# A transformer-like layer on one core: both token halves normed first, and modulated in turn after each half of the modulation vectors

## The chip, the core and the metric

The kernel runs on one core of a Trainium2 chip. TensorE (PE) multiplies matrices, VectorE (DVE) and ScalarE (ACT) do elementwise work, GpSimd (POOL) helps with a few subtractions, and SyncE (SP) issues the DMA transfers from one queue. The metric is device time in microseconds; three runs of the kernel before gave 1233.12 to 1235.85 with a median of 1234.98.

## The reference

One layer of a streaming encoder, 1024 tokens of width 1024, all in float32. Only its beginning matters here:

```python
mod = silu(c) @ w_ada + b_ada                      # 6 vectors of 1024
shift1, scale1, gate1, shift2, scale2, gate2 = split(mod, 6)
u = layer_norm(x) * (1 + scale1) + shift1
proj = u @ w_in                                    # columns: rq rk rv rg gq gk gv gg glr
m = token_mixer(proj) @ w_out                      # retention heads and gated linear attention
x = layer_norm(alpha * x + gate1 * m, ln1)
...                                                # second modulation, relu(.)**2 feed-forward, second norm
```

`c` is a single vector, so `mod` is a matrix-vector product that reads all of `w_ada`, 25 MB.

## The kernel before

The kernel is written as a program whose instructions a scheduler puts in order on each engine; the order of the code, priorities and the buffers that tiles share decide it. `tc.issue_after(i)` lets what is written inside it be placed only behind instruction i. Every engine then runs its own queue strictly in that order, and semaphores hold an instruction until what it reads has been written.

Tokens are worked on in two halves h of 512 (four tiles of 128 each), features in eight blocks k of 128. `load_x` (line 295) issues eight loads of 256 KB for a half; `ln_x` (307) takes statistics on VectorE, gets the scale `rs` and bias `nb` for four tiles at once (a square root on ScalarE in the middle), writes the normed tiles `xh` (six on ScalarE, two on VectorE), transposes them on TensorE in eight groups of four (line 331) and copies each group to SBUF on ScalarE as `xT[k][h]` (334).

The first modulation (shift1 and scale1) is computed in two halves b of 512 columns each, by `ada_first` (251). A half loads 16 weight tiles of 256 KB. For the first `share` of the eight row blocks, TensorE multiplies the tile by a column of silu(c) (line 262); the rest are summed on VectorE into `acc` (235 and 237), and one matmul adds the partitions of that sum. ScalarE copies the two result rows (264), four tiny transposes turn them (267), and VectorE adds the bias into `mod` (269). With SHARES = ((8, 0), (6, 0)), half 0 has nine such matmuls and half 1 has eight.

`modulate_all(h, b)` then makes, for the four feature blocks of half b, `uf` = xT * scale + shift on VectorE (341) and splits it into a rounded part `uh` (cast on ScalarE, 204) and a remainder `ul` (subtraction on VectorE, 205). A float32 product is three matmuls of such parts (`mm3`, 210 to 212). `begin(h, keys)` starts the products of three key and query blocks (gq 0, gk 0, gq 1) with the first four feature blocks of a half: 36 matmuls of 512 columns. The other four blocks follow in `feature_major` (430) when the second half of the modulation is done, and after gq 0 and gk 0 come the gv products (`values_and_gate`, 454).

PSUM is used through two pools of four buffers each, `pj` and `mx`; the transposes and the modulation sums take theirs from `mx`. The code that sets the order of the beginning stands at lines 405 to 422.

Of the kernel before, what the change touches and what calls it, by code (L numbers as in the profile page):

```python
# [78 lines left out]
def layer_kernel(ctx: ExitStack, tc, x, c, w_ada, b_ada, w_in, ret_norm_w, gla_gate_w, gla_gate_b,  # L79
# [27 lines left out]
    def S(shape=(P, HALF), dt=F32, n="s"):  # L107
        tag, bufs = TAGS.get(n, ("S", None))
        return sp.tile(list(shape), dt, tag=tag, name=nm(n), bufs=bufs)
# [7 lines left out]
    def pjt(shape=(P, HALF)):  # L117
        return pj.tile(list(shape), F32, tag="pj", name=nm("pj"))

    def mxt(shape=(P, HALF)):  # L120
        return mx.tile(list(shape), F32, tag="mx", name=nm("mx"))

    def small(n, tag, bufs=4):
        return sm.tile([P, n], F32, tag=tag, name=nm(tag))
# [51 lines left out]
    def row_rsqrt(dst, var, n=1):  # L176

        v, y, t = small(n, f"qv{n}"), small(n, f"qy{n}"), small(n, f"qt{n}")
        A.activation(y, var, AF.Sqrt, bias=eps)
        V.tensor_scalar(out=v, in0=var, scalar1=EPS, scalar2=None, op0=ALU.add)  # L180
        yield
        V.reciprocal(out=y, in_=y)
        yield
        if n == 1:

            V.tensor_scalar(out=t, in0=y, scalar1=-0.5, scalar2=y, op0=ALU.mult, op1=ALU.mult)
            V.tensor_scalar(out=t, in0=t, scalar1=v, scalar2=None, op0=ALU.mult)
            yield
            V.tensor_scalar(out=dst, in0=t, scalar1=1.5, scalar2=y, op0=ALU.add, op1=ALU.mult)
            return  # L190
        V.scalar_tensor_tensor(out=t, in0=y, scalar=-0.5, in1=y, op0=ALU.mult, op1=ALU.mult)
        V.tensor_tensor(out=t, in0=t, in1=v, op=ALU.mult)
        yield
        V.scalar_tensor_tensor(out=dst, in0=t, scalar=1.5, in1=y, op0=ALU.add, op1=ALU.mult)

    def stats(parts, mv):
        bs = small(6 * len(parts), f"bs{len(parts)}")
        for i, a in enumerate(parts):
            V.bn_stats(out=bs[:, 6 * i:6 * i + 6], in_=a)
        V.bn_aggr(out=mv, in_=bs)  # L200
# [6 lines left out]
    def mm3(ps, lh, ll, rh, rl, first, last, partial=False):  # L207


        T.matmul(ps, lhsT=lh, rhs=rh, start=first, stop=False, skip_group_check=partial)  # L210
        T.matmul(ps, lhsT=lh, rhs=rl, start=False, stop=False, skip_group_check=partial)  # L211
        T.matmul(ps, lhsT=ll, rhs=rh, start=False, stop=last, skip_group_check=partial)  # L212
# [10 lines left out]
    def ada_load(cols, get):  # L223
        ws = []
        for k in range(NK):
            w = get()
            nc.sync.dma_start(out=w, in_=wa[k, :, cols:cols + HALF])
            ws.append(w)
        return ws

    def ada_sum(ws, ks):
        acc = S(n="acc")
        for n, k in enumerate(ks):
            if n == 0:
                V.tensor_scalar(out=acc, in0=ws[k], scalar1=sc[:, k:k + 1], scalar2=None, op0=ALU.mult)
            else:
                V.scalar_tensor_tensor(out=acc, in0=ws[k], scalar=sc[:, k:k + 1], in1=acc, op0=ALU.mult, op1=ALU.add)
        return acc
# [12 lines left out]
    def ada_first(b, shares):  # L251


        ps = mxt()
        todo = []
        for i, share in ((1, shares[0]), (0, shares[1])):
            ws = ada_load(1024 * i + HALF * b, ada_early)
            todo += [(pick2[:, 16 * i + 2 * k:16 * i + 2 * k + 2], ws[k]) for k in range(share)]
            if share < NK:
                todo.append((pick2[:, 32 + 2 * i:34 + 2 * i], ada_sum(ws, range(share, NK))))  # L260
        for n, (l, r) in enumerate(todo):
            yield T.matmul(ps[0:2, :], lhsT=l, rhs=r, start=n == 0, stop=n == len(todo) - 1)
        r = S(n="acc")
        A.copy(out=r[0:2, :], in_=ps[0:2, :])
        pt = mxt((P, 4, 2))
        for j in range(4):
            T.transpose(out=pt[:, j, :], in_=r[0:2, j * P:(j + 1) * P], identity=ident[0:2, 0:2])
        for i in range(2):
            V.scalar_tensor_tensor(out=mod[:, 8 * i + 4 * b:8 * i + 4 * b + 4], in0=pt[:, :, i], scalar=float(i),
                                   in1=colT[:, 8 * i + 4 * b:8 * i + 4 * b + 4], op0=ALU.add, op1=ALU.add)  # L270
# [24 lines left out]
    def load_x(h):  # L295
        xs = []
        for j in range(4):
            t = 4 * h + j
            pr = []
            for q in range(2):  # L300
                a = S(n="x")
                nc.sync.dma_start(out=a, in_=x[0, t * P:(t + 1) * P, q * HALF:(q + 1) * HALF])
                pr.append(a)
            xs.append(pr)
        return xs

    def ln_x(h, xs):
        mv = small(8, "mvx", bufs=2)
        for j in range(4):
            stats(xs[j], mv[:, 2 * j:2 * j + 2])  # L310
        mvv = mv.rearrange("p (j two) -> p j two", two=2)
        rs = small(4, "rsx", bufs=2)
        nb = small(4, "nbx", bufs=2)
        var = small(4, "varx", bufs=2)
        V.tensor_copy(out=var, in_=mvv[:, :, 1])
        for _ in row_rsqrt(rs, var, 4):
            pass
        V.scalar_tensor_tensor(out=nb, in0=mvv[:, :, 0], scalar=-1.0, in1=rs, op0=ALU.mult, op1=ALU.mult)
        hs = [[None, None] for _ in range(4)]
        for q in range(2):  # L320
            for j in range(4):
                a = hs[j][q] = S(n="xh")
                if q == 0 and j % 2:
                    V.tensor_scalar(out=a, in0=xs[j][q], scalar1=rs[:, j:j + 1], scalar2=nb[:, j:j + 1],
                                    op0=ALU.mult, op1=ALU.add)
                else:
                    A.activation(a, xs[j][q], AF.Identity, bias=nb[:, j:j + 1], scale=rs[:, j:j + 1])
        for k in range(NK):
            ps = mxt()
            for j in range(4):  # L330
                T.transpose(out=ps[:, j * P:(j + 1) * P], in_=hs[j][k // 4][:, (k % 4) * P:(k % 4 + 1) * P],
                            identity=ident)
            xT[k][h] = S(n="xT")
            A.copy(out=xT[k][h], in_=ps)
# [4 lines left out]
    def modulate(k, h, src, sh, s1):  # L339
        u = S(n="uf")  # L340
        V.tensor_scalar(out=u, in0=src, scalar1=s1, scalar2=sh, op0=ALU.mult, op1=ALU.add)
        uh[k][h] = S(dt=F32R, n="uh")
        ul[k][h] = S(dt=F32R, n="ul")
        split(u, uh[k][h], ul[k][h], lo_eng=V)
# [21 lines left out]
    for kind in ("gqk0", "gqk1", "rqk0", "rqk1", "rqk2", "rqk3"):  # L366
        i = int(kind[3])
# [13 lines left out]
    def take(key, ahead=1):  # L381

        n = order.index(key)
        for u in order[:n + 1 + ahead]:
            if u not in loaded:
                loaded[u] = load_w(*W[u])
        return loaded[key]

    def begin(h, keys):

        for key in keys:
            w = take(key, 0)
            begun.setdefault(key, [None, None])[h] = ps = pjt() if key[1] == 0 else mxt()
            for k in range(4):
                mm3(ps, w[0][k], w[1][k], uh[k][h], ul[k][h], k == 0, False)

    begun = {}
    SHARES = ((8, 0), (6, 0))
    EARLY_KEYS = (("gq", 0), ("gk", 0), ("gq", 1))

    def modulate_all(h, b):
        for k in range(4 * b, 4 * b + 4):
            modulate(k, h, xT[k][h], mod[:, k:k + 1], mod[:, 8 + k:9 + k])

    xs = load_x(0)
    steps = ada_first(0, SHARES[0])
    for _ in range(SHARES[0][0]):
        i = next(steps)
    with tc.issue_after(i.ins):
        ln_x(0, xs)  # L410
    for _ in steps:
        pass
    modulate_all(0, 0)
    begin(0, EARLY_KEYS)
    ln_x(1, load_x(1))
    for i in ada_first(1, SHARES[1]):
        pass
    modulate_all(1, 0)
    with tc.issue_after(i.ins):
        begin(1, EARLY_KEYS)  # L420
    for h in range(2):
        modulate_all(h, 1)
    nc.sync.dma_start(out=cst1, in_=cst[:, C_DEC:])
# [732 lines left out]
    ys, x1, xs = {}, {}, {}  # L1156
# [79 lines left out]
    for t in range(NT):  # L1236
        tile_steps = final(t)
        for step in range(4):
            i = next(tile_steps)
# [34 lines left out]
```

## Time and profile before

| | us |
|---|---|
| median of three runs | 1234.98 |
| profiled execution | 1232.21 |
| its span | 1230.4 |
| TensorE busy | 1170.1 (95%) |
| VectorE busy | 959.5 (78%) |
| ScalarE busy | 495.4 (40%) |

The page lists for each engine how long it was busy in the span, and then the span in 40 slices; the timeline lists single instructions in order of time; the windows give the busy time of an engine in stretches. PEclk is the clock that TensorE was granted, as a share of full speed (2.4 GHz). The first slice of 31 us and the last hold the least TensorE work; the DMA engines are busy for over 90% of the first.

### The profile page before, as it was taken

How to read it: one execution, taken by the hardware profiler on the slowest of the kernel's cores; microseconds unless marked ns; L12 is line 12 of the kernel's file. 1: busy time of each engine (PE TensorE's matmuls, PEld its weight loads, DVE VectorE, ACT ScalarE, POOL GpSimd, SP SyncE). 2: the span in 40 equal slices, each digit the busy share in tenths (PEclk: the TensorE clock that was granted, in tenths of full speed). 3: DMA queues.
4: the chain of work that ended last, by engine and by line, in shares of the span. 5: the costliest groups of instructions: out<-in, count | busy, mean ns of one | idle time of the engine just before them, and what ended most of it. 6: DMA issues, size and time to landing. Idle time of an engine off the chain costs nothing. (4 is left out here: it accounts for less than half of the span.)

```text
span 1230.4 us, 19534 instructions
## 1 busy us (share of the span) xinstructions
PE 1170.1 (95%) x7195; PEld 973.8 (79%) x7195; DVE 959.5 (78%) x1870; ACT 495.4 (40%) x887; POOL 162.1 (13%) x141
## 2 busy tenths in 40 slices
PE   5899889989999999999989999999999999999995
PEld 2588788759989999888867887888887888878784
DVE  6885888888776763698898799864856976897886
ACT  5514333211222232223754457756655363431132
POOL 0000332041000000000000000000002131243146
PEclk9999999989999999999999999999999999999998
DMA  9793211110110313181236688563656275378442
GB/s 314 248 332 120 87 61 36 28 27 18 44 36 25 101 64 95 60 273 44 94 112 208 209 306 308 195 210 130 224 188 204 78 254 156 114 236 299 174 137 103
DMA packets 124129, 183.13 MB, mean 149 GB/s; under 512 B 12337, under 2 KB 52482, under 8 KB 124034
## 3 DMA queue, kind: packets, MB, share of 16 engines
q1 hardware_dynamic: 124034, 181.89, 44.5%
q8 instruction: 56, 0.92, 0.3%
q14 instruction: 39, 0.32, 0.1%
HBM read 136.76 MB, written 45.09 MB: 148 GB/s over the span
## 5 line engine op out<-in xcount | busy, mean ns | idle before, releaser
L211 PE MATMUL pj<-wl,uh 128*128 128x256 f32 (+1 forms) x512 | 146.8, 287 | 1.0 <-DVE wl L205 1.0
L212 PE MATMUL pj<-wh,ul 128*128 128x256 f32 (+1 forms) x512 | 146.9, 287 | 0.0
L210 PE MATMUL pj<-wh,uh 128*128 128x256 f32 (+1 forms) x512 | 146.5, 287 | 0.3 <-ACT wh L204 0.3
L210 PE MATMUL pj<-uhp,w1h 128*128 128x512 f32 x256 | 100.9, 396 | 1.7 <-ACT w1h L204 1.1
L210 PE MATMUL pj<-bh,ah 128*128 128x512 f32 x256 | 99.9, 391 | 1.6 <-DVE yacc L1100 1.6
L211 PE MATMUL pj<-ulp,w1h 128*128 128x512 f32 x256 | 100.4, 393 | 0.1
L212 PE MATMUL pj<-uhp,w1l 128*128 128x512 f32 x256 | 100.4, 393 | 0.0
L211 PEld LDWEIGHTS pj<-wl,uh 128*128 128x128 f32 x512 | 98.2, 192 | 2.2 <-DVE wl L205 1.2
L212 PE MATMUL pj<-bh,al 128*128 128x512 f32 x256 | 99.7, 390 | 0.0
L211 PE MATMUL pj<-bl,ah 128*128 128x512 f32 x256 | 99.7, 389 | 0.0
L210 PEld LDWEIGHTS pj<-wh,uh 128*128 128x128 f32 x512 | 98.0, 192 | 1.2 <-ACT wh L204 0.7
L212 PEld LDWEIGHTS pj<-wh,ul 128*128 128x128 f32 x512 | 98.2, 192 | 1.0 <-issue 0.7
L205 POOL TENSOR_TENSOR al<-rh,ah 128x512 fp32r<-128x512 f32 x17 | 26.9, 1580 | 537.4 <-PE pj L212 474.5
L210 PE MATMUL mx<-bh,ah 128*128 128x512 f32 x192 | 75.6, 395 | 3.5 <-ACT bh L204 2.4
L210 PE MATMUL mx<-uhp,w1h 128*128 128x512 f32 x192 | 75.6, 395 | 2.9 <-ACT w1h L204 2.7
L211 PE MATMUL mx<-bl,ah 128*128 128x512 f32 x192 | 75.4, 393 | 1.5 <-POOL bl L205 1.3
L212 PE MATMUL mx<-uhp,w1l 128*128 128x512 f32 x192 | 75.7, 395 | 0.0
L211 PE MATMUL mx<-ulp,w1h 128*128 128x512 f32 x192 | 75.6, 394 | 0.0
L212 PE MATMUL mx<-bh,al 128*128 128x512 f32 x192 | 75.3, 392 | 0.0
L205 DVE TENSOR_TENSOR w1l<-raw,w1h 128x512 fp32r<-128x512 f32 x80 | 54.7, 686 | 25.6 <-ACT w1h L204 16.1
L210 PE MATMUL pj<-uh,wh 128*128 128x512 f32 x176 | 71.3, 406 | 1.6 <-ACT uh L204 1.6
L204 ACT CAST ah<-rh 128x512 fp32r<-128x512 f32 x84 | 51.9, 618 | 51.3 <-PE pj L211 21.4
(256 smaller groups left out, 2874.8 us busy)
## 6 DMA issues: line engine op xcount, KB each, us to landing
raw<-in_w_ff SPq DMA_DIRECT2D x140, 256.0 KB, 4.3
ada<-in_w_ada SPq DMA_DIRECT2D x96, 256.0 KB, 5.4
rh<-hid SPq DMA_DIRECT2D x84, 256.0 KB, 3.7
hid<-c SPq DMA_DIRECT2D x54, 256.0 KB, 2.6
st<-in_w_in SPq DMA_DIRECT2D x52, 256.0 KB, 3.0
hid<-m SPq DMA_DIRECT2D x30, 256.0 KB, 2.2
hid<-kl SPq DMA_DIRECT2D x28, 256.0 KB, 3.0
hid<-kh SPq DMA_DIRECT2D x28, 256.0 KB, 2.9
```

Source lines behind the costliest of these rows:

```text
L204: A.copy(out=hi, in_=src)
L205: (lo_eng or G).tensor_tensor(out=lo, in0=src, in1=hi.bitcast(F32), op=ALU.subtract)
L210: T.matmul(ps, lhsT=lh, rhs=rh, start=first, stop=False, skip_group_check=partial)
L211: T.matmul(ps, lhsT=lh, rhs=rl, start=False, stop=False, skip_group_check=partial)
L212: T.matmul(ps, lhsT=ll, rhs=rh, start=False, stop=last, skip_group_check=partial)
```

## The change

The two halves of x are loaded and normed ahead of everything else. Then comes the first half of the modulation, the modulation of both token halves by it, each followed by its 36 products, and then the second half of the modulation. The `issue_after` orderings of this part are gone. Functions and shares stay as they are; after.py's lines from 411 on have numbers that are 6 lower.

```diff
-    xs = load_x(0)
-    steps = ada_first(0, SHARES[0])
-    for _ in range(SHARES[0][0]):
-        i = next(steps)
-    with tc.issue_after(i.ins):
-        ln_x(0, xs)
-    for _ in steps:
+    xs = [load_x(h) for h in range(2)]
+    for h in range(2):
+        ln_x(h, xs[h])
+    for _ in ada_first(0, SHARES[0]):
         pass
-    modulate_all(0, 0)
-    begin(0, EARLY_KEYS)
-    ln_x(1, load_x(1))
-    for i in ada_first(1, SHARES[1]):
+    for h in range(2):
+        modulate_all(h, 0)
+        begin(h, EARLY_KEYS)
+    for _ in ada_first(1, SHARES[1]):
         pass
-    modulate_all(1, 0)
-    with tc.issue_after(i.ins):
-        begin(1, EARLY_KEYS)
     for h in range(2):
         modulate_all(h, 1)
```

How the queues change is seen at three places. In the names a number tells tiles of one kind apart: `ada` is a weight tile of the modulation, `acc` a VectorE sum of such tiles or the copied result row, `xh` a normed tile, `xT` a transposed block, `wh` and `wl` the two parts of a weight.

TensorE, around the sums of the first modulation half, before:

```order
L262 MATMUL mx_113<-ada_114,pick_92 2x512
...
L262 MATMUL mx_113<-ada_128,pick_92 2x512
L331 MATMUL mx_210<-keep,xh_194 128x128
...
L331 MATMUL mx_259<-keep,xh_208 128x128
L262 MATMUL mx_113<-acc_146,pick_92 2x512
L267 MATMUL mx_269<-keep,acc_267 128x2 x4
L210 MATMUL pj_312<-uh_278,wh_302 128x512
```

and now:

```order
L331 MATMUL mx_176<-keep,xh_160 128x128
...
L331 MATMUL mx_225<-keep,xh_174 128x128
L331 MATMUL mx_279<-keep,xh_263 128x128
...
L331 MATMUL mx_328<-keep,xh_277 128x128
L262 MATMUL mx_335<-ada_336,pick_92 2x512
...
L262 MATMUL mx_335<-acc_368,pick_92 2x512
L267 MATMUL mx_388<-keep,acc_386 128x2 x4
L210 MATMUL pj_431<-uh_397,wh_421 128x512
```

The eight sums stood ahead of half 0's transposes; now the transposes of both halves (`xh_160` to `xh_174` are half 0, `xh_263` to `xh_277` half 1) stand ahead of all nine.

TensorE, around the sums of the second modulation half, before:

```order
L331 MATMUL mx_487<-keep,xh_436 128x128
L262 MATMUL mx_494<-ada_495,pick_92 2x512
...
L262 MATMUL mx_494<-acc_530,pick_92 2x512
L210 MATMUL pj_580<-uh_558,wh_302 128x512
...
L267 MATMUL mx_549<-keep,acc_547 128x2 x4
L211 MATMUL pj_580<-ul_565,wh_302 128x512
...
L212 MATMUL mx_606<-uh_576,wl_353 128x512
L210 MATMUL pj_312<-uh_621,wh_308 128x512
```

and now:

```order
L212 MATMUL mx_481<-uh_415,wl_472 128x512
L210 MATMUL pj_518<-uh_496,wh_421 128x512
...
L212 MATMUL mx_544<-uh_514,wl_472 128x512
L262 MATMUL mx_557<-ada_558,pick_92 2x512
...
L262 MATMUL mx_557<-acc_593,pick_92 2x512
L267 MATMUL mx_612<-keep,acc_610 128x2 x4
L210 MATMUL pj_431<-uh_621,wh_427 128x512
```

Half 1's 36 products stood between the sums and the first product of the second half of the features (`uh_621`); now they stand ahead of the sums, and between the sums and `uh_621` there are only the four tiny transposes.

ScalarE, behind the copies of half 0's transposes, before:

```order
L334 COPY xT_264<-mx_259 128x512
L204 CAST wh_302<-st_300 128x512
L264 COPY acc_267<-mx_113 2x512
L204 CAST wh_308<-st_306 128x512
L204 CAST uh_278<-uf_276 128x512
```

and now:

```order
L334 COPY xT_230<-mx_225 128x512
L179 ACTIVATE qy_62_254<-varx_251,keep 128x4
L327 ACTIVATE xh_263<-x_113,nbx_250,rsx_249 128x512
...
L334 COPY xT_284<-mx_279 128x512
...
L334 COPY xT_333<-mx_328 128x512
L204 CAST wh_421<-st_419 128x512
...
L264 COPY acc_386<-mx_335 2x512
L204 CAST uh_397<-uf_395 128x512
```

Half 1's square root, six normed tiles and eight copies, and six casts of weights, now stand between half 0's last copy and the copy of the modulation's result row. On SP, 14 of the 16 x loads stand ahead of the first weight load of the modulation, and the last x load is the 21st of the large loads.

## Rows read from the trace of the kernel before

**Rows 1.** Windows: start and end, length, PE busy, PEclk, DMA share, GB/s.

```profile
0.00:75.00 75.00, 56.88 (x228) 0.95 0.89 295
75.00:300.00 225.00, 208.72 (x2445) 0.98 0.24 76
```

**Rows 2.** Timeline, 0 to 26 us: start, length, engine, line, operation.

```profile
6.88 10.91 SPq L227 DMA_DIRECT2D ada<-in_w_ada  x15
...
12.70 0.69 DVE L199 BATCH_NORM_STATS2 bs<-x 128x6 f32<-128x512 f32 x1 [0.66 <-DMA x<-in_x]
...
15.20 0.30 ACT L179 ACTIVATE qy<-varx,keep 128x4 f32<-128x4 f32 x1
...
15.53 0.18 DVE L182 RECIPROCAL qy<-qy 128x4 f32<-128x4 f32 x1 [1.49 <-ACT qy L179]
...
16.33 0.16 DVE L318 SCALAR_TENSOR_TENSOR nbx<-mvx,rsx 128x4 f32<-128x4 f32 x1
16.53 4.34 ACT L327 ACTIVATE xh<-x,nbx,rsx 128x512 f32<-128x512 f32 x6 [1.03 <-DVE nbx L318]
...
18.10 0.48 DVE L235 TENSOR_SCALAR acc<-ada,keep 128x512 f32<-128x512 f32 x1 [0.57 <-DMA ada<-in_w_ada]
...
21.61 4.01 ACT L334 COPY xT<-mx 128x512 f32<-128x512 f32 x8 [0.74 <-PE mx L331]
```

**Rows 3.** Timeline of PE, 12 to 39 us.

```profile
12.13 8.85 PE L262 MATMUL mx<-ada,pick 128*2 128x512 f32 x16 [5.64 <-DVE bs L199]
...
20.92 3.72 PE L331 MATMUL mx<-keep,xh 128*128 128x128 f32 x32
...
24.56 1.02 PE L262 MATMUL mx<-acc,pick 128*2 128x512 f32 x2
...
28.54 0.50 PE L210 MATMUL pj<-uh,wh 128*128 128x512 f32 x1 [1.56 <-ACT uh L204]
...
38.86 0.39 PE L212 MATMUL mx<-uh,wl 128*128 128x512 f32 x1
```

**Rows 4.** Timeline, half 1's norm to the first gv product.

```profile
41.48 0.16 DVE L318 SCALAR_TENSOR_TENSOR nbx<-mvx,rsx 128x4 f32<-128x4 f32 x1
...
42.60 5.66 PE L331 MATMUL mx<-keep,xh 128*128 128x128 f32 x32 [3.36 <-ACT xh L327]
...
48.19 5.31 PE L262 MATMUL mx<-ada,pick 128*2 128x512 f32 x12
...
55.15 0.50 PE L210 MATMUL pj<-uh,wh 128*128 128x512 f32 x1
...
61.30 0.39 PE L210 MATMUL mx<-uh,wh 128*128 128x512 f32 x1
...
64.03 0.39 PE L210 MATMUL pj<-uh,wh 128*128 128x512 f32 x1
...
74.91 0.28 PE L210 MATMUL pj<-wh,uh 128*128 128x272 f32 x1
```

**Rows 5.** Windows of PE around its gaps: busy, PEclk, DMA share, GB/s.

```profile
12.00:14.00 2.00, 1.87 (x3) 1.00 1.06 404
29.00:33.00 4.00, 3.64 (x10) 0.57 1.08 362
...
43.00:47.00 4.00, 3.95 (x21) 0.57 0.57 171
```

**Rows 6.** Lines of DVE, 0 to 75 us: count, busy us, mean ns, idle before.

```profile
L237 DVE SCALAR_TENSOR_TENSOR acc<-ada,keep,acc 128x512 f32<-128x512 f32 x23 | 17.3, 751 | 0.8 <-DMA ada<-in_w_ada 0.3
L205 DVE TENSOR_TENSOR ul<-uf,uh 128x512 fp32r<-128x512 f32 x16 | 10.9, 686 | 0.0
...
L341 DVE TENSOR_SCALAR uf<-xT,keep 128x512 f32<-128x512 f32 x16 | 8.3, 542 | 0.0
```

**Rows 7.** Waits of PE, 75 to 330 us: total, times, longest.

```profile
PE mx L549 <- DVE ke L570: 11.8, 8, 5.7
...
PE pj L211 <- DVE wl L205: 1.0, 1, 1.0
```

## The prediction

> **What bounds the kernel now.** I read the page's busy shares first, then the busy time of TensorE by stage, then the timeline of the first 75 us in order of time, the granted clock there, and last the waits of TensorE afterwards. TensorE is the bound: it is busy for 95% of the span, and VectorE, next to it, for 78%; from 0 to 75 us TensorE is busy only 56.9 us [rows 1]. The change touches that stretch alone. From the first gv product on (74.91 us, [rows 4]; pj_820 on the PE queue in both programs) TensorE runs nearly the same order of instructions, so the question is how much later or earlier that product starts. I call this moment G.
>
> Before G the reader should see three things. TensorE starts the column sums of the first modulation half (line 262) at 12.13 us as the weights land, while ScalarE still norms token half 0 [rows 2, 3]. The products of half 0 run from 28.54 to 39.09 us (the last starts at 38.86, plus one spacing) [rows 3]. Then TensorE waits 3.4 us for half 1's norm, transposes it from 42.60, sums the second modulation half from 48.19, and runs half 1's products from 55.15 to 64.03, under which the second modulation is worked out, so that nothing waits at 64.03 [rows 4].
>
> **The change part by part.** No instruction is added or dropped; all of the cost is order. Times are from the span's start.
>
> *Loads.* Half 1's eight x loads now stand ahead of most of the first modulation weights. On SP the last x load is the 21st load of 256 KB; before, half 0's last was the 9th, used at 12.70 us, and the 17th was used at 18.10, so a load takes about 0.70 us (15 issues took 10.91, or 0.73 each) [rows 2]. The last x then lands near 12.70 + 12 x 0.70 = 21.1 us, and the last weight of the first half, 13 loads later, near 30.2 instead of by 24. Six us later by itself; the next step hides it.
>
> *Half 1's norm, on ScalarE.* It has one queue: six normed tiles of half 0 (16.53 to 20.87), eight copies of the transposes (4.01 us, now from 20.9 on, as the transposes no longer stand behind the sums), then half 1's square root (0.30), and VectorE's 0.96 us from reciprocal to bias [rows 2]: 26.2 us. The data (21.1 plus 1.1 for the statistics) is there earlier, so ScalarE sets it.
>
> *The wait that is added, on TensorE.* The first sums now stand behind all 64 transposes. In half 1 of before, the first sum started 6.55 us after the bias was done (41.64 to 48.19 [rows 4]); the same instructions stand between them now, so the first sum starts at 26.2 + 6.55 = 32.7. Nine sums at 0.87 (eight took 6.96, from 48.19 to 55.15 [rows 4]) end at 40.5, where before they ended at 25.58 [rows 3]. Behind them wait the copy on ScalarE, the modulation on VectorE and every product on TensorE. From the end of the sums to the first product is 2.96 us (25.58 to 28.54 [rows 3]): 43.5, which is 15.0 later than before.
>
> *What TensorE need no longer do after that.* Half 1's transposes and the 3.4 us wait ahead of them are gone from the middle. Both halves' products follow each other: 72 at 0.2275 us (twelve took 2.73, from 61.30 to 64.03 [rows 4]) are 16.4. Half 0 took 10.55 us for 36, which is 2.4 more than 36 x 0.2275; 1.7 of that is clock, the rest the wait for the first operands. I charge it once: 43.5 + 16.4 + 2.4 = 62.3. VectorE supplies a 128x512 operand in 0.54 + 0.69 us [rows 6] against three products of 0.68 us in all for each of three keys, so it does not bind.
>
> *Second modulation.* Its loads wait for buffers that the first sums free (33 to 40 us), and land long before 62.3. Eight sums take 7.0: 69.3. Before, half 1's products covered what follows; now nothing does. The gap is the 2.96 us above and one 0.75 us sum that VectorE's queue has ahead of the modulation [rows 6]: 73.0.
>
> *The rest of the three keys before G.* 49 products, 11.1 us, plus 1.7 for the clock: 85.8. The same from VectorE: 8 x 0.54 + 8 x 0.69 + 2 x 0.75 = 11.3 from 71.9 on, then 11 products, 2.5: 85.7. I take 85.8, against 74.91: 10.9 later.
>
> *After G.* TensorE waited 1.0 us near 91 us for the low half of a weight, which stands on VectorE behind sums of later modulation vectors [rows 7]. VectorE is about three sums ahead at G now, so I give back 0.9, between nothing and 1.0. Sum: 10.0 us. On the profiled 1232.2 us (span 1230.4 and 1.8 around it) that is 1242.2; the median of the timed runs lies 2.8 above the profiled one, so 1234.98 + 10.0 = **1245.0**.
>
> **The clock.** After the two gaps of before the granted clock was 0.57 on average for 4 us each time (29 to 33 and 43 to 47), mostly at 0.5, that is 1.2 GHz [rows 5]: 4 x 0.43 = 1.7 us lost each. After the change the gaps stand at 40.5 and 69.3 and I charge 1.7 in each; the bounds are 0, and 2.4, all that half 0 lost. From 12 to 14 us it was 1.00 although TensorE had done nothing but one transpose before [rows 3, 5]. The Trainium skill (TensorE: Matmul & The Clock Gate, What's actually happening) says the opposite of such a start: an idle engine is at the half rate by default, and work releases it. By that rule half 0's transposes, which are now the first work after a long idle time, would take twice their 3.72 us, and as they run beside ScalarE's copies the sum would be some 0.4 us more, an estimate from [rows 2, 3]; by the row it stays at 10.0. The measurement decides.
>
> **The rivals.**
> 1. *TensorE isn't held by the transposes* as long as I think: half 1's norm is done sooner, and the sums end when their data has landed (30.2 + 0.75 + 0.87 = 31.8). All is then 8.7 us earlier: 1236.3. Against it: ScalarE's queue, whose durations are all in [rows 2]. Something in between, 1237 to 1241, is likelier than the whole.
> 2. *The clock stays up* in both gaps, since each has a few small matmuls in it: 3.4 us less, 1241.6. Against it: both gaps of before, with the same small matmuls in the first, lost it.
> 3. *It costs more*: VectorE or ScalarE, which now modulate both halves in one go between casts of weights, become the bound of the two product stretches, as in the 0.7 us that half 0 lost beside the clock; 2 us in each: 1249.
> 4. *Not slower*: the lost time is won back after G. TensorE sits idle 225 - 208.7 = 16.3 us between 75 and 300 us [rows 1], 11.8 of it at scores that wait for VectorE's ke [rows 7]. If VectorE's lateness there comes from work that isn't shifted (the sums of the later modulation vectors), a TensorE that comes 11 us later finds it done, and from 11 won back on the time is no longer slower; all 16.3 (0.9 of it is in the sum) would give 1229.6. For it: VectorE is the releaser. Against it: ke is made of gates that come from TensorE's own products after G, so that the chain shifts with it.
>
> **How the numbers follow.** My forecast 0.62, rival 1 0.12, rival 2 0.12, rival 3 0.10, rival 4 0.04. The range runs from 1239.5 (which leaves out rival 4 and half of rival 1) to 1250.0. About 0.2%, 2.5 us, is what a measurement of this kernel can tell from no change. Faster by more is 0.03, from rival 4; within it 0.05, the rest of rival 4 and the full form of rival 1; slower 0.92.
>
> **What would show it.** In the profile after: the 64 transposes ahead of the first sum; that sum near 32.7 us and the first product near 43.5; a gap of some 3.7 us near 69 with the granted clock at half behind it; G near 86. A first sum before 30, or no half clock after the gaps, would make single terms wrong; a G near 86 with a total within 3 us of before would make the reading of the rest wrong, and a G below 77 the whole.

## The result and the profile after

The changed kernel took 1242.66 us (median of four runs, 1240.21 to 1243.65) against 1234.32 for the kernel before beside it; the ratio is 1.0071 with a 95% interval of 1.0049 to 1.0093, that is 8.8 us (6.0 to 11.5) more; the two medians by themselves are 8.3 apart. 1245.0 had been predicted, 10.0 more than the 1234.98 it was reckoned from. The span of the profiled execution is 1238.1 us, 7.7 more than before.

The first view is the timeline of TensorE up to the first gv product (start, length, engine, line, operation, and in brackets the idle time before it with what ended it); it answers to [rows 3, 4].

```profile
16.62 6.41 PE L331 MATMUL mx<-keep,xh 128*128 128x128 f32 x32 [11.68 <-ACT xh L327]
26.05 5.17 PE L331 MATMUL mx<-keep,xh 128*128 128x128 f32 x32 [3.02 <-ACT xh L327]
31.14 7.03 PE L262 MATMUL mx<-ada,pick 128*2 128x512 f32 x16
38.01 1.02 PE L262 MATMUL mx<-acc,pick 128*2 128x512 f32 x2
39.70 0.41 PE L267 MATMUL mx<-keep,acc 2*128 2x2 f32 x4 [0.66 <-ACT acc L264]
41.66 0.73 PE L210 MATMUL pj<-uh,wh 128*128 128x512 f32 x2 [1.55 <-ACT uh L204]
...
59.99 5.31 PE L262 MATMUL mx<-ada,pick 128*2 128x512 f32 x12
...
70.18 1.22 PE L210 MATMUL pj<-uh,wh 128*128 128x512 f32 x2 [2.09 <-ACT uh L204]
...
82.89 0.28 PE L210 MATMUL pj<-wh,uh 128*128 128x272 f32 x1
```

The order is the forecast one. All 64 transposes stand ahead of the first sum at 31.14 us, the first product comes at 41.66, the second sums follow the 72 products at 59.99 and leave a gap that ends at 70.18, and G, the first gv product, is at 82.89: 7.98 us later than the 74.91 of [rows 4].

The next view is the busy time by stretch (start and end, length, busy time with the count, granted clock, DMA share, GB/s), first around the gaps (beside [rows 5]), then up to and behind 75 us (beside [rows 1]).

```profile
20.00:21.00 1.00, 1.00 (x6) 1.00 1.04 383
...
27.00:28.00 1.00, 1.00 (x6) 0.50 1.21 302
...
29.00:30.00 1.00, 1.00 (x11) 1.00 1.18 309
...
41.00:46.00 5.00, 4.34 (x11) 0.66 0.92 287
70.00:73.50 3.50, 3.32 (x8) 0.53 0.90 294
```

```profile
75.00:300.00 225.00, 210.28 (x2419) 0.98 0.26 80
```

Half 0's transposes, the first work after 11.7 us of nothing, have 1.00 beside them, but they ran at half clock (1.2 GHz). From 20 to 21 us TensorE was busy all the time, with 6 of them. That is as many as from 27 to 28 us, where the granted clock was 0.50; from 29 to 30 us, at 1.00 (2.4 GHz), it was 11. The trace has no record of the granted clock ahead of 22.11 us, and a window shows 1.00 where there is none. In the trace of the kernel before the records begin at 15.84 us, so the 1.00 from 12 to 14 us in [rows 5] is not a measurement either. After each of the three later gaps the granted clock was 0.5 for a while: behind the one that ends at 26.05, at 41.66 and at 70.18. Behind 75 us TensorE sat idle 225 - 210.28 = 14.7 us, 16.3 before; the window now begins with products that stood ahead of it before, so this is no gain.

The waits of TensorE from 70 us on (total, number of times, longest) answer to [rows 7].

```profile
PE mx L543 <- DVE ke L564: 11.9, 8, 5.8
...
PE pj L211 <- DVE wl L205: 0.3, 1, 0.3
```

The wait for ke (L543 now, L549 before) is 11.9 us as against 11.8, so nothing of the delay is won back there. From G to the end of the span there are 1238.1 - 82.89 = 1155.2 us, and 1230.4 - 74.91 = 1155.5 before. The whole difference arises ahead of G.

### The profile page after: what moved, and what is told of

Read it like the earlier page. It is cut to its first block, busy times and chain, and to the rows that moved or that the text cites. A ratio compares the mean times of both kernels' runs of the same rounds, so it can differ in the third digit from the quotient of the medians.

```text
span 1238.1 us, 19564 instructions
## 1 busy us (share of the span) xinstructions
PE 1172.3 (95%) x7195; PEld 978.3 (79%) x7195; DVE 958.3 (77%) x1870; ACT 496.3 (40%) x887; POOL 162.3 (13%) x141
## 4 chain that ended last, share of the span: by engine, by line
PE 77%; DVE 13%; DMA 4%; issue 3%; ACT 2%; SPq 1%; POOL 0%; DVEq 0%; ACTq 0%; POOLq 0%
PE pj L211 17%; PE pj L212 16%; PE pj L210 16%; PE mx L211 7%; PE mx L210 7%; PE mx L212 7%; PE mx L262 1%; DVE acc L237 1%; PE mx L543 1%; DMA ada<-in_w_ada 1%; DMA x<-in_x 1%; DVE t L637 1%; DVE ke L564 1%; DMA st<-in_w_out 1%; DVE t L638 1%
```

## The experiments

Every kernel below was also timed beside the kernel before. Its G is the first gv product in its profile, and it locates the change better than the times do: in these sets single runs of the kernel before ranged from 1227.6 to 1240.0 us. The kernel before and the three below that keep its loads and its opening (e10, e11, e12) started half 0's products at 28.5 to 29.9 us and half 1's transposes at 42.6 to 44.0, so the same opening varies by 1.4 us from profile to profile, and I read a difference in G of up to that as none.

| kernel | G, us | ratio to before, 95% interval |
|---|---|---|
| before | 74.91 | 1 |
| changed | 82.89 | 1.0071 (1.0049 to 1.0093) |
| e1_t1_later | 82.19 | 1.0062 (1.0026 to 1.0097) |
| e2_cover | 78.60 | 1.0036 (1.0015 to 1.0057) |
| e4_loads | 78.20 | 1.0032 (1.0004 to 1.0059) |
| e5_fill_after | 88.11 | 1.0117 (1.0075 to 1.0159) |
| e6_fill_own_tile | 80.35 | 1.0053 (1.0028 to 1.0079) |
| e10_before_no_cover | 85.14 | 1.0045 (1.0026 to 1.0064) |
| e13_t1_behind_products | 83.90 | 1.0061 (1.0039 to 1.0082) |
| e8_x1_after_ada | 73.93 | 1.0009 (0.9991 to 1.0028) |
| e9_x1_after_ada_fill | 73.83 | 1.0022 (1.0003 to 1.0040) |
| e11_before_fill | 74.94 | 0.9992 (0.9970 to 1.0014) |
| e12_before_pool_fill | 75.54 | 0.9989 (0.9975 to 1.0003) |

**e1_t1_later: half 1's transposes behind the sums.** In the changed kernel:

```diff
-    for h in range(2):
-        ln_x(h, xs[h])
-    for _ in ada_first(0, SHARES[0]):
+    ln_x(0, xs[0])
+    for i in ada_first(0, SHARES[0]):
         pass
+    with tc.issue_after(i.ins):
+        ln_x(1, xs[1])
```

> The changed kernel, but half 1's 32 transposes may only stand behind the nine sums of the first modulation half on TensorE; loads and everything behind stay as in the changed kernel. Theory (the hold: the sums wait behind half 1's transposes): the sums start when half 0's transposes end, near 23 us instead of 31.1, and end with the last weight near 31; half 1's transposes fill the gap behind them; first product near 36, first gv product (G) near 75.5 instead of 82.9, so 7.4 us less than the changed kernel, a ratio to before of 1.0005. Rival (the loads: the weights of the modulation land too late for an earlier start): the sums end near 38 as now, G stays within 1 us of 82.9, ratio 1.0065.

Measured, TensorE's timeline:

```profile
23.14 7.03 PE L262 MATMUL mx<-ada,pick 128*2 128x512 f32 x16
32.23 1.55 PE L262 MATMUL mx<-acc,pick 128*2 128x512 f32 x2 [2.06 <-DVE acc L237]
...
34.96 5.86 PE L331 MATMUL mx<-keep,xh 128*128 128x128 f32 x32
42.14 0.73 PE L210 MATMUL pj<-uh,wh 128*128 128x512 f32 x2 [1.32 <-ACT uh L204]
```

Neither expectation describes what happened, though the rival's number came true. The sums did start at 23.14 us, 8.0 earlier. But the VectorE part of them held the last one until 32.23: on VectorE it stands behind half 1's bias and ran from 25.85 to 32.17 without a wait for weights. Half 1's transposes then stood in front of the products, and behind them the first product waited another 1.32 us for ScalarE, which copies the transposes first. The first product came at 42.14, no earlier than in the changed kernel, and G moved by 0.7. So the hold was real, but taking it away from the sums only moved it to the products.

**e2_cover: the cover given back.** In the changed kernel, with half 1's first products behind the second sums again:

```diff
-    for h in range(2):
-        modulate_all(h, 0)
-        begin(h, EARLY_KEYS)
-    for _ in ada_first(1, SHARES[1]):
+    modulate_all(0, 0)
+    begin(0, EARLY_KEYS)
+    for i in ada_first(1, SHARES[1]):
         pass
+    modulate_all(1, 0)
+    with tc.issue_after(i.ins):
+        begin(1, EARLY_KEYS)
```

> The changed kernel, but half 1's first 36 products stand behind the sums of the second modulation half again, as they did before. Theory (the cover: nothing lies over the second modulation's copy, transposes and VectorE work): the gap of 3.2 us near 67 us and the 1.7 us of half clock behind it go, first product still near 41.7, G near 78.1 instead of 82.9, ratio to before 1.0026. Rival (the gap is VectorE's supply and only moves): G within 1 us of 82.9, ratio 1.0065.

```profile
60.00 0.41 PE L267 MATMUL mx<-keep,acc 2*128 2x2 f32 x4
...
78.60 0.28 PE L210 MATMUL pj<-wh,uh 128*128 128x272 f32 x1
```

```profile
60.00:63.00 3.00, 3.00 (x17) 1.00 0.14 45
```

The tiny transposes at 60.00 have no idle time in front of them and stand among half 1's products; the gap and its half clock are gone and G is 78.60, 4.3 earlier, against 4.8 expected. The ratio, 1.0036, fits the theory's 1.0026 and its interval leaves out the rival's 1.0065.

**e4_loads: the loads alone.** In the kernel before, only half 1's x loads move ahead of the weights of the modulation:

```diff
-    xs = load_x(0)
+    xs, xs1 = [load_x(h) for h in range(2)]
...
-    ln_x(1, load_x(1))
+    ln_x(1, xs1)
```

> The kernel before, but half 1's eight x loads are written right behind half 0's, ahead of the modulation weights; the code's order of the compute is that of before. Theory (the order of the compute costs, not that of the loads): the first product comes some 5.5 us later than before's 28.5, since the weights land later, but the 3.4 us wait for half 1's norm and the 1.7 us of half clock behind it go: G near 74.5 against 74.9, ratio 1.000 (0.998 to 1.002). Rival (the loads are the cost): G 5 to 8 us later than before, ratio 1.004 to 1.0065.

```profile
16.86 9.61 PE L262 MATMUL mx<-ada,pick 128*2 128x512 f32 x16 [7.81 <-DMA ada<-in_w_ada]
...
31.36 1.02 PE L262 MATMUL mx<-acc,pick 128*2 128x512 f32 x2 [1.25 <-DVE acc L237]
...
36.18 0.79 PE L210 MATMUL pj<-uh,wh 128*128 128x512 f32 x1 [1.61 <-ACT uh L204]
...
47.89 3.65 PE L331 MATMUL mx<-keep,xh 128*128 128x128 f32 x32
...
78.20 0.28 PE L210 MATMUL pj<-wh,uh 128*128 128x272 f32 x1
```

```profile
40.00:42.00 2.00, 2.00 (x6) 0.50 1.05 387
```

G lies between the two, 3.3 us later than before. The sums wait for weights until 16.86 instead of 12.13 [rows 3], and the first product is 7.6 us later than in [rows 3] (5.5 expected). Half 1's transposes then follow the products with no wait and at full clock (3.65 us against 5.66 in [rows 4]), which gives back some 5 us; the half clock behind the longer first gap lasts to 42 us and takes part of that again. The code's order of the compute is that of before, but the scheduler used the earlier loads: two of half 1's normed tiles (30.91 to 32.49 us) now stand ahead of the copy of the first sums on ScalarE, and TensorE waited 1.79 us for that copy instead of 1.00. So the 3.3 is the price of the loads together with what the queues made of them. The profiled execution was the slowest of this kernel's ten (1244.16 us, median 1237.19), but that loss lies behind G, from where it took 1164.2 us as against 1155.5.

These kernels make a path of single edits from before to the changed kernel: the loads, 74.91 to 78.20, +3.3; both halves' transposes ahead of the sums (e2_cover), 78.20 to 78.60, +0.4; the cover of the second modulation taken away, 78.60 to 82.89, +4.3. Each step has the spread of some 1.4 us named above. The ratios give the same split, with wider intervals: 1.0032, 1.0036 and 1.0071.

**e13_t1_behind_products: the other path.** To see whether the hold costs when there is no cover, the changed kernel with half 1's norm behind half 0's products:

```diff
-    for h in range(2):
-        ln_x(h, xs[h])
-    for _ in ada_first(0, SHARES[0]):
+    ln_x(0, xs[0])
+    for i in ada_first(0, SHARES[0]):
         pass
-    for h in range(2):
-        modulate_all(h, 0)
-        begin(h, EARLY_KEYS)
+    modulate_all(0, 0)
+    begin(0, EARLY_KEYS)
+    with tc.issue_after(i.ins):
+        ln_x(1, xs[1])
+    modulate_all(1, 0)
+    begin(1, EARLY_KEYS)
```

> The changed kernel with half 1's norm and transposes written behind half 0's first 36 products; the x loads stay ahead of everything, and nothing covers the second modulation. First reading (the sums' wait behind half 1's transposes is a cost of its own): first product at 36.2 us instead of 41.7, 5.5 less, and 3.7 back for transposes that now stand between the products: G near 81.1 instead of 82.9, ratio to before 1.005. Second reading (half 1's transposes have to be done somewhere, and behind half 0's products nothing covers half 1's own modulation either): 2.1 us of wait and 1.5 us of half clock more behind the transposes, G at 84.5 to 86.4, ratio 1.008 or more.

```profile
35.65 1.22 PE L210 MATMUL pj<-uh,wh 128*128 128x512 f32 x2 [1.55 <-ACT uh L204]
...
46.79 3.65 PE L331 MATMUL mx<-keep,xh 128*128 128x128 f32 x32
52.00 0.73 PE L210 MATMUL pj<-uh,wh 128*128 128x512 f32 x2 [1.55 <-ACT uh L204]
...
83.90 0.28 PE L210 MATMUL pj<-wh,uh 128*128 128x272 f32 x1
```

The first product is 6.0 us earlier than in the changed kernel, as the first reading has it; then 3.65 us of transposes and a 1.55 us wait for half 1's own operands come back at 46.79 to 52.00, and G is 83.90, 1.0 later. Part of the rest is the clock: behind the first gap it was 0.50 in every us from 35 to 40, while in the changed kernel the stretch from 41 to 46 us has 0.66. G falls between the two readings, nearer to the second. With the +0.4 above, the hold's net cost is nothing that these traces can tell.

**e10_before_no_cover: the cover taken from the kernel before.**

```diff
-    for i in ada_first(1, SHARES[1]):
-        pass
     modulate_all(1, 0)
-    with tc.issue_after(i.ins):
-        begin(1, EARLY_KEYS)
+    begin(1, EARLY_KEYS)
+    for _ in ada_first(1, SHARES[1]):
+        pass
```

> The kernel before, with one change only: half 1's first 36 products are written ahead of the sums of the second modulation half, so that nothing lies over the second modulation's copy and VectorE work. Theory (the cover is worth the same in either kernel): products from 48.2 to 56.4 us, sums to 63.4, a gap of 3.2, half clock behind it, G near 79.3 instead of 74.9, ratio 1.0036. Rival (the cover mattered only after the other edits): G within 1 us of 74.9, ratio 1.000.

```profile
43.95 5.76 PE L331 MATMUL mx<-keep,xh 128*128 128x128 f32 x32 [3.26 <-ACT xh L327]
51.85 1.22 PE L210 MATMUL pj<-uh,wh 128*128 128x512 f32 x2 [2.13 <-ACT uh L204]
...
72.33 1.22 PE L210 MATMUL pj<-uh,wh 128*128 128x512 f32 x2 [2.09 <-ACT uh L204]
...
85.14 0.28 PE L210 MATMUL pj<-wh,uh 128*128 128x272 f32 x1
```

The theory's cost is there (the gap that ends at 72.33, with 12.8 us to G behind it, as in the changed kernel), and it is larger than expected: 10.2 us in this profile. In the kernel before, the second sums cover something themselves, half 1's first modulation on VectorE and ScalarE; without them TensorE waits 2.13 us ahead of 51.85 and has half the clock behind it (0.50 from 52 to 55 us, which is 1.5 us). And this execution was 1.4 us late already at half 1's transposes. Its times moved less, by 0.45% or 5.6 us (3.2 to 7.9); which part of the 10.2 is this one execution's stays open.

**e5_fill_after and e6_fill_own_tile: the clock in the gaps.** The changed kernel with identity matmuls that nobody reads:

```diff
+    def fill(px, i, n):
+        with tc.issue_after(i.ins):
+            for _ in range(n):
+                T.matmul(px[:, P:2 * P], lhsT=ident, rhs=ident, start=True, stop=True)
...
-        pt = mxt((P, 4, 2))
+        px = mxt()
+        pt = px[:, 0:8].rearrange("p (j two) -> p j two", two=2)
+        fill(px, t, 5)
...
+        fill(px, t, (10, 15)[b])
```

> The changed kernel with 5 idle-time matmuls (128x128 of the identity, never read) between the sums and the four tiny transposes of each modulation half, and 10 and 15 behind these. Theory (the gaps cost twice, by the wait and by the half clock behind it): granted clock 1.00 behind both gaps instead of 0.5 for 3.3 us each, G near 79.6 instead of 82.9, ratio to before 1.004. Rival (the half clock doesn't come from the gap, or such matmuls don't keep it up): clock 0.5 as now behind both, G within 0.5 us of 82.9 or up to 1 us later, ratio 1.0065 or more.

VectorE's timeline, and windows of TensorE in the same kernel (its lines are 9 higher here):

```profile
43.75 0.23 DVE L278 SCALAR_TENSOR_TENSOR keep<-mx,keep 128x4 f32<-128x4 f32 x2 [2.56 <-PE mx L254]
```

```profile
45.50:46.50 1.00, 0.96 (x4) 1.00 0.81 254
...
76.60:78.00 1.40, 1.37 (x5) 1.00 1.05 404
```

The clock stayed at 1.00, as the theory has it, but G came 5.2 us later. The read of the modulation vectors (L278) waited for the last of the extra matmuls, since they write the same tile. That is the experiment's own fault, mended in the next, where the extra matmuls have a PSUM tile of their own, with 2 ahead of the tiny transposes and 5 and 7 behind.

```diff
-        pt = px[:, 0:8].rearrange("p (j two) -> p j two", two=2)
-        fill(px, t, 5)
+        fill(px, t, (2, 2)[b])
+        pt = mxt((P, 4, 2))
...
-        fill(px, t, (10, 15)[b])
+        fill(px, t, (5, 7)[b])
```

> The changed kernel with matmuls of the identity that nobody reads, into a PSUM tile of their own: 2 between the sums and the tiny transposes of each modulation half, 5 and 7 behind these. Theory (the gap itself lowers the clock, and the 5.2 us that the first such kernel lost were VectorE's wait for a tile that the extra matmuls wrote): first product at 41.7 us as in the changed kernel, granted clock 1.00 behind both gaps, G (the first gv product) near 80.0 instead of 82.9 (1.55 and 1.23 us less), ratio to before 1.004. Rival (the extra matmuls themselves take TensorE's time, or so few don't keep the clock): G at 82.9 or later, ratio 1.0065 or more.

```profile
41.93 0.74 PE L210 MATMUL pj<-uh,wh 128*128 128x512 f32 x2 [0.24 <-ACT uh L204]
...
68.89 0.74 PE L210 MATMUL pj<-uh,wh 128*128 128x512 f32 x2 [0.33 <-ACT uh L204]
...
80.35 0.28 PE L210 MATMUL pj<-wh,uh 128*128 128x272 f32 x1
```

```profile
41.50:46.00 4.50, 4.26 (x19) 1.00 0.85 266
...
70.00:73.50 3.50, 3.50 (x16) 1.00 0.93 269
```

The first product comes when it did (41.93), the clock behind it is 1.00 instead of 0.66 and behind the second gap 1.00 instead of 0.53, and G is 80.35, so that the half clock behind these two gaps cost the changed kernel 2.5 us. These are not 2.5 of the 8.0: the kernel before has half clock behind its own two gaps [rows 5], and what the fills are worth there is seen in e11 below. The tile was the fault of e5_fill_after: here the read of the modulation vectors came at 40.41 us, while the extra matmuls ran on to 41.69. The times allow it (1.0053) without proving it, since the interval holds 1.0065 too.

**e8, e9, e11, e12: can both be beaten?** Four kernels that start from the kernel before. First (e8), half 1's x loads right behind the first weights of the modulation; second (e9), the same with fills in the first gap, `(2, 0)[b]` and `(6, 0)[b]` of them.

```diff
-    for _ in range(SHARES[0][0]):
+    for n in range(SHARES[0][0]):
         i = next(steps)
+        if n == 0:
+            xs1 = load_x(1)
...
-    ln_x(1, load_x(1))
+    ln_x(1, xs1)
```

> The kernel before, but half 1's x loads are written right behind the first modulation half's weight loads, ahead of the products' weights. Theory (loads cost what they are put ahead of): the first sums are not late, so the first product stays within 1.5 us of 28.5; half 1's norm is done in time, so that the 3.4 us wait ahead of its transposes and the 1.7 us of half clock behind it shrink or go: G at 71 (70 to 73) instead of 74.9, ratio 0.997. Rival (the products' weights, now later, become the wait): G within 1 us of 74.9 or later, ratio 1.000.

> The kernel just described (half 1's x loads behind the first weights of the modulation), with 2 identity matmuls that nobody reads between the first half's sums and the tiny transposes, and 6 behind these, into a PSUM tile of their own. Theory: the clock is 1.00 behind the first gap, G 1.7 us earlier than without them, near 69.5, ratio 0.9955. Rival (they cost what they save): G as without them.

The waits of TensorE from 10 to 80 us in the first of them:

```profile
PE pj L212 <- DVE wl L205: 2.7, 1, 2.7
PE pj L210 <- ACT wh L204: 2.5, 1, 2.5
```

The rival was right: the wait for half 1's norm is gone, and 5.2 us of waits for the products' own weights stand in its place. The second shows the same with its clock kept: 1.00 from 28 to 32 us (0.58 in the first), but then 3.0 us of waiting for a weight, and 0.50 again from 35 to 37 us. G is 1.0 and 1.1 us earlier, within the spread, and neither time is better than before; the second kernel's interval lies above 1.

Third (e11), the kernel before with fills in both gaps (2 and 6 around the tiny transposes, 11 behind half 0's products); fourth (e12), 5 instead of 11 and three weight remainders moved to GpSimd.

```diff
-    begin(0, EARLY_KEYS)
+    i = begin(0, EARLY_KEYS)
+    fill(mxt(), i, 11)
...
-            split(w, th, tl, lo_eng=V)
+            split(w, th, tl, lo_eng=G if kk == 4 and k and len(loaded) < 3 else V)
```

> The kernel before with identity matmuls that nobody reads, into PSUM tiles of their own, in its two gaps: 2 between the first half's sums and the tiny transposes, 6 behind these, 11 behind half 0's 36 products, ahead of half 1's transposes. Theory (each gap costs 1.7 us of half clock behind it): granted clock 1.00 from 29 to 33 us and from 43 to 47, G near 71.7 instead of 74.9, ratio 0.9975. Rival (half 0's products are held by VectorE's operands and weights as much as by the clock, and half 1's transposes by ScalarE's copies): less than 1 us, ratio 0.9995.

> The same with 5 instead of 11 identity matmuls behind half 0's products, and with the remainders of three weight tiles that are needed only from 57 us on (second half of the first three keys) subtracted on GpSimd, which is idle, instead of VectorE: VectorE's statistics of half 1 end 1.8 us earlier, so the 3.4 us wait for half 1's norm is 1.6. Theory: G near 70, ratio 0.996. Rival (the statistics wait for the loads of x, which land when they did): G as in the kernel with 11.

The third kernel's windows and timeline of TensorE:

```profile
29.00:33.00 4.00, 3.54 (x15) 1.00 1.08 362
...
43.00:47.00 4.00, 3.97 (x21) 0.58 0.58 170
```

```profile
37.92 2.62 PE L254 MATMUL mx<-keep 128*128 128x128 f32 x22
42.59 5.71 PE L340 MATMUL mx<-keep,xh 128*128 128x128 f32 x32 [2.05 <-ACT xh L336]
```

The clock behind the first gap was kept at 1.00 (0.57 in [rows 5]), and half 0's products ended at 37.92 instead of 39.1. It bought nothing at G: half 1's transposes start at 42.59, against 42.60 in [rows 4], because they wait for half 1's norm. Behind 2.05 us of idle time the clock was half again. In the fourth kernel half 1's statistics ended at 39.76 us, 0.1 earlier than in the kernel before (39.84; 1.8 had been expected), and its bias came at 42.19 (41.48 in [rows 4]). VectorE waited for no load of x on the way, so the rival's reason isn't seen. What is seen is that VectorE's instructions were longer beside GpSimd's subtractions, here the scale next to the third of them:

```profile
40.93 1.22 DVE L194 SCALAR_TENSOR_TENSOR rsx<-qt,qy 128x4 f32<-128x4 f32 x1
42.19 0.16 DVE L327 SCALAR_TENSOR_TENSOR nbx<-mvx,rsx 128x4 f32<-128x4 f32 x1
```

```profile
40.88 1.26 POOL L205 TENSOR_TENSOR wl<-st,wh 128x512 fp32r<-128x512 f32 x1 [7.30 <-DMA ada<-in_w_ada]
```

The same instruction took 0.16 us in the kernel before (41.28), and three `uf` took 2.30 us beside the first subtraction, 1.46 in the third kernel. No run separates this from other causes. Both kernels take the same time as before within their intervals. No kernel was found that is clearly better than both.

## Why the prediction was right, and where its terms were off

- **The place and the sign.** All of the change arises ahead of G and nothing is won back behind it, as forecast. Rival 4 (the wait for ke) is refuted by 11.9 against 11.8 us.
- **The added wait.** The first sum was forecast for 32.7 and came at 31.14. The bias of half 1 was ready at 25.1 instead of 26.2, and from there to the sum it took 6.0 us instead of 6.55. ScalarE's queue was the reason given, and its timeline shows it, with the square root of half 1 behind half 0's copies (first fence), 2.1 us after its input was written on VectorE (second fence; the second row is the bias):

```profile
20.00 3.95 ACT L334 COPY xT<-mx 128x512 f32<-128x512 f32 x8
23.81 0.34 ACT L179 ACTIVATE qy<-varx,keep 128x4 f32<-128x4 f32 x1
25.18 4.34 ACT L327 ACTIVATE xh<-x,nbx,rsx 128x512 f32<-128x512 f32 x6 [1.03 <-DVE nbx L318]
```

```profile
21.57 0.17 DVE L315 COPY varx<-mvx 128x4 f32<-128x4 f32 x1
...
24.98 0.16 DVE L318 SCALAR_TENSOR_TENSOR nbx<-mvx,rsx 128x4 f32<-128x4 f32 x1
```

- **"Six us later by itself; the next step hides it."** This is the step that was sized wrong. The loads are not hidden: they put the first product 7.6 us later by themselves (e4_loads), so that of the 13.1 us by which the changed kernel's first product is late, some 5.5 are left for the transposes (6.0 in e13_t1_behind_products). And the hold I put in the centre costs nothing clear of the spread in the end (+0.4 and -1.0 on the two paths), for the transposes have to stand somewhere, and ahead of the products they also spare the wait in the middle. The sum was not hurt, because it charged the two as one delay of the first product and credited the middle separately.
- **The middle and the products.** 18.8 us were charged from the first product to the second sums (16.4 + 2.4), 18.33 were taken. The credit for half 1's transposes and the wait ahead of them held: nothing stands between the 72 products.
- **The second modulation.** "Now nothing does": the gap was 70.18 less the end of the sums (59.99 + 6.96 = 66.95), 3.2 us, against 3.7 charged, and giving the cover back was worth 4.3 with its clock. With the loads (3.3) it makes up nearly all of the path; which of the two is larger the spread leaves open.
- **The clock.** Charged at 1.7 for each gap, 3.4. The fills recovered 2.5 us. Rival 2 (the clock stays up) is refuted by 0.66 and 0.53. My reading of 1.00 from 12 to 14 us, which I held against the rule, was wrong, for the trace has no record of the clock there. The rows show the lower level at the start of both kernels. One transpose took 426 ns from 16.6 to 21 us, as from 26 to 28.5 (425 ns, at 0.50), and 276 ns from 29.3 to 31 (at 1.00); in the kernel before one matmul of the first sums took 1041 ns from 12 to 14 us and 592 from 18 to 20.9. The weighed rule of the Trainium skill (TensorE: Matmul & The Clock Gate, What's actually happening), that an idle engine starts at half rate, agrees with half 0's transposes, which took 6.41 us against 3.72 [rows 3], and with all three gaps later on. It cost the sum nothing that shows: ScalarE, which sets the pace there, copied their results right behind its normed tiles and without a gap (20.00 to 23.95).
- **Rival 3** (VectorE or ScalarE become the bound) did not happen; the terms came out below the charges, not above.
- **Rival 1** was half true: unheld, the sums end 5.3 us earlier (39.03 against 32.23 + 1.55 = 33.78 in e1_t1_later), not 8.7, and that alone bought 0.7 at G.
- **After G** 0.9 was given back. The wait named went from 1.0 to 0.3, and from G to the end 0.3 us were saved in the two profiled executions. In the other profiles that stretch runs from 1153.7 us (e1_t1_later) to 1166.2 (e9_x1_after_ada_fill), so 0.3 is no measurement.

The sum of the terms was 10.9 at G and 8.0 were measured. Every stage was charged somewhat too high: 1.6 up to the first sum, 0.3 from there to the first product, 0.5 for the products, 0.5 for the second sums and the gap, 0.1 for the last stage. The give-back on top made the forecast 10.0, and 8.8 (6.0 to 11.5) were measured. That it brought the forecast nearer to the time is luck: no trace confirms the 0.9.

## What to carry to other kernels

When an edit moves a long chain ahead of a bound engine's work, follow what the moved chain would have covered or waited for in its old place as carefully as the new wait: here the wait in front cost almost nothing net, and the cover that was lost behind and the loads moved ahead cost about half each. A wait that stands later in the stage absorbs every gain in front of it (half 0's products ended 1.2 us earlier and nothing followed), so look for the last wait of a stage before tuning its first. Peel a change into a chain of kernels one edit apart and compare one marker in their traces; the marker resolved some 1.4 us where the times could not resolve 3. And look at the rows beside a granted clock: at the start of a trace it can be a figure without a record.

## What the runs showed of the hardware

- TensorE's first real work, after 11.7 us of idle time, ran at half clock (426 ns for a transpose, 276 at 1.00), although the windows show 1.00 there: the records of the clock begin at 22.11 us. After gaps of 3.0 us (0.50 from 27 to 28 us) and less in the middle of the program it was half as well.
- A few small matmuls in a gap kept the clock behind it at 1.00 (0.66 and 0.53 without them, e6_fill_own_tile). In e9_x1_after_ada_fill 3.0 us of idle time behind them brought 0.50. In e5_fill_after 1.8 and 2.1 us of idle time behind them did not lower it; in e11_before_fill 2.05 us did (0.58 from 43 to 47 us). What tells these apart stays open.
- A VectorE read of a PSUM tile waited for the last matmul that wrote any column of the tile. In the changed kernel the read starts 0.44 us after the first tiny transpose (39.70 to 40.14), in e5_fill_after 2.87 us (40.88 to 43.75), right behind the last extra matmul. It is a semaphore of the program that holds the read; whether the chip needs it is not shown.
- VectorE's instructions took longer beside GpSimd's subtractions in e12_before_pool_fill: 1.22 us instead of 0.16, and 2.30 instead of 1.46 for three. That the one causes the other is not shown by a run of its own.
